# Row gathers moved from the routing to later blocks, and the gate product made for two expert blocks at a time, in a hybrid encoder layer

## The chip, the cores and the metric

The kernel runs on one core of a Trainium2 chip. The metric is the device time of one launch in microseconds; the kernel before takes 1673.27 us (median of three runs, 1672.91 to 1676.97). In the profile PE is TensorE (matrix products), DVE is VectorE, ACT is ScalarE, POOL is GpSimd and SP is the engine that issues most DMAs. PEld is PE's weight load.

## The reference, cut to what matters

One layer of an encoder on 512 tokens of width 1024. A mixing half (a long convolution and a gated recurrence) ends in a residual stream `h`. What this change touches is the second half, a retrieval over 16384 experts of one neuron each:

```python
def peer(x, wq, keys, u_tab, v_tab):
    q = (x @ wq).reshape(B, L, PEER_HEADS, 2, D_HALF)
    s = jnp.einsum('blhpd,hpkd->blhpk', q, keys)
    ts, ti = lax.top_k(s, K)
    ...
    experts = e1 * N_KEYS + e2
    g = jax.nn.softmax(cs, axis=-1)
    ...
        act = jax.nn.gelu(jnp.einsum('td,tkd->tk', xt, u_tab[et])) * gt
        return jnp.einsum('tk,tkd->td', act, v_tab[et])
```

Each token picks 8 x 16 experts; its output is the sum over them of gelu(x . u) times a gate g times v. The layer ends with a normalisation.

## The kernel before

**Two ways for the tokens.** For the first 384 tokens (`TD`) the kernel takes all 16384 experts, in 128 blocks of 128: a u block multiplies the block's u rows with the tokens (24 matmuls on PE into `ps_e`), ACT takes the gelu (L1019), a gate matrix that is zero for unchosen experts is multiplied in, and a v block adds the product times the block's v rows to the PSUM tiles `ob` (18 matmuls, L1045). For the other 128 tokens it fetches the 128 chosen u rows and later the 128 chosen v rows of each token from DRAM with indirect DMAs on POOL ("gathers", L1160, one row for each of 128 tokens, tile `rows`); DVE makes a dot product for each u gather (L1194, tile `junk`) and a multiply-add for each v gather (L1215, `acc2`, shown as `acc`). `GB` is 6, so five gathers are in flight ahead of the one in use.

**Weights.** Every matrix operand is fp16 in two parts. `w_load` fetches a block (tile `wf`, SP), `split` makes the high part on ACT (L119) and the rest on DVE (L120), tile `wh`, of which there are four; three `wf` buffers, six once the pool `gp` is open.

**Order of the work.** Every engine executes its instructions in the order in which the program wrote them. The loop over `self.seq` in `peer` writes u blocks 0 to 95 + LV, then a v block and a u block by turns, then v blocks alone. v blocks are taken in the order 96 to 127, then 0 to 95 (`vorder`). While the gates are still being worked out ("the routing": top-16 searches, one-hot matrices `oh` and `og` for eight tokens at a time, and matmuls `ps_gt` that turn them into the gate matrix, which ACT copies to `stg` and SP writes to DRAM, `gd`), each u block pulls a portion of the routing:

```python
                    self.pull(*self.PACE)
                    self.bud[0] -= 1.3 * gathers(self.GRATE[0])
```

`pull` writes routing instructions until 4.2 us of estimated DVE time (or of ACT time) are used up; each gather step is charged at 1.3 us. `gathers(rate)` adds the rate to a credit and writes one gather step for each whole unit; it starts once the row numbers `gidx` are there. When the routing is written out, the loop closes its pools, opens `vp` and the `ob` tiles, and asks for the first gate block (`gload`, four DMAs `gin<-gd`); from there the rate is `GRATE[1]` = 1.5 for each u and v block, and from the 33rd v block on it is (268 - steps done)/(E0 - 5), with E0 = 96.

**A v block's operand.** `pmul` multiplies the gelu (tile `sin`, reloaded from DRAM, or `hs`, still in SBUF) with the gates `gin` into `pf` (DVE, L1000); `phi` rounds it to fp16 on ACT (L1007, `pt`), `plo` makes the residue on DVE (L1011). At v block i the program writes `phi(i+2)`, `pmul(i+3)`, gathers, `plo(i+2)`. The last three v blocks' matmuls (`VT`) are written behind everything else, tile after tile of `ob`, each followed by `final`, the closing normalisation and the output's DMA.

Of the kernel before, what the change touches and what calls it, by code (L numbers as in the profile page):

```python
# [66 lines left out]
class Kernel:  # L67
# [276 lines left out]
    def front(self, xt, acc):  # L344
# [536 lines left out]
    def peer(self, acc):  # L881
        nc, tc, a = self.nc, self.tc, self.a
        E0, LV, VT = self.E0, self.LV, self.VT
        ctx = ExitStack()
# [87 lines left out]
        vp = None  # L972
        order = self.vorder
        gin, sin, pt, pf = {}, {}, {}, {}
        gs = {}

        def gload(k, q):
            if k < 128 // EB:
                b = order[EB * k] // EB
                if b not in gin:  # L980
                    gin[b] = vp.tile([128, NCH, EB, CH], F32, name="gin", bufs=2)
                cs = slice(q * NCH // 4, (q + 1) * NCH // 4)
                nc.sync.dma_start(gin[b][:, cs].rearrange("p c e t -> p c (e t)"),
                                  gd[cs, :, CH * EB * b:CH * EB * (b + 1)].rearrange("c p n -> p c n"))

        def sload(i):
            if i < 128 and order[i] < E0 and i % 2 == 0:
                b = order[i] // 2
                sin[b] = vp.tile([128, 2, TD], F32, name="sin", bufs=4)
                nc.sync.dma_start(sin[b], sd[b])  # L990

        def pmul(i):
            if i >= 128:
                return
            e = order[i]
            if i % EB in (3, 5, 7, 9):
                gload(i // EB + 1, (i % EB - 3) // 2)
            sload(i + 6)
            f = pf[i] = vp.tile([128, TD], F32, name="pf", bufs=2)
            nc.vector.tensor_tensor(f.rearrange("p (c t) -> p c t", c=NCH),  # L1000
                                    sin[e // 2][:, e % 2, :].rearrange("p (c t) -> p c t", c=NCH),
                                    gin[e // EB][:, :, e % EB, :], OP.mult)

        def phi(i):
            if i < 128:
                pt[i] = vp.tile([128, 2, TD], F16, name="pt", bufs=4)
                nc.scalar.activation(pt[i][:, 0, :], pf[i], AF.Copy)  # L1007

        def plo(i):
            if i < 128:  # L1010
                nc.vector.tensor_tensor(pt[i][:, 1, :], pf.pop(i), pt[i][:, 0, :], OP.subtract)  # L1011

        def gelu(e, ps):
            if e % 2 == 0:
# [39 lines left out]
        rate = None  # L1054
        for pos, (kind, e) in enumerate(seq):
            if kind == "u":
# [14 lines left out]
                if vp is None and (route not in self.bgq or e == E0 - 3):  # L1071
# [7 lines left out]
                    vp = ctx.enter_context(tc.tile_pool(name="vp", bufs=1, side="right"))  # L1079
# [9 lines left out]
                continue  # L1089
            i, vi = vi, vi + 1  # L1090
            if i == 0:
                for k in range(3):
                    pmul(k)
                    if k < 2:
                        phi(k)
                        plo(k)
            phi(i + 2)
            pmul(i + 3)
            if i >= 128 - E0:
                if rate is None:  # L1100
                    rate = (268 - self.gsteps) / (E0 - 5.0)
                gathers(rate)
            else:
                gathers(self.GRATE[1])
            plo(i + 2)
            w = self.w_get(u0 + pos)
            pp = pt.pop(i)
            if i >= 128 - VT:
# [7 lines left out]
            k = i - (128 - E0) - 20  # L1116
            if 0 <= k < 24:
                tt, c = divmod(k, 8)
# [24 lines left out]

    VT = 3
    E0 = 96
    LV = 5
    PACE = (4.2, 4.2)
    TB = 8
    GRATE = (0.8, 1.5)
    LAG = 2  # L1150
    GB = 6

# [388 lines left out]
```

## Time and profile before

| | before |
|---|---|
| runs | 1672.91, 1673.27, 1676.97 us |
| profiled execution | 1672.62 us, its span 1670.8 us |
| PE busy | 1610.5 us (96%) |
| DVE busy | 1407.0 us (84%) |
| ACT busy | 767.9 us (46%) |
| POOL busy | 379.6 us (23%) |
| moved by DMA | 435.06 MB, mean 260 GB/s |

The first u block begins at 578.5 us, the gathers at 674.6 us. In the order of PE's instructions the last `ps_gt` stands behind u block 89 and ends at 1004.5 us; the first v block begins at 1057.5 us, behind u block 101; from there to 1663.5 us v blocks follow. A share of busy time over the span says little here, since the stages differ; the rows below are taken stage by stage. In the rows of a stretch (a window), each engine has its busy time and its instructions, then PE's granted clock (1.00 is full), the mean busy share of the 16 DMA engines, and the GB/s they moved.

### The profile page before, as it was taken

The page shows a single profiled execution, that of the slowest core. Times are in us where ns is not written, and L with a number is a line of the kernel's source. Part 1 is how long each engine was busy: PE and PEld are TensorE (multiplying, and loading weights), DVE is VectorE, ACT ScalarE, POOL GpSimd, SP SyncE. Part 2 cuts the span into 40 slices and gives each one's busy share as a digit, 9 for nine tenths or more (in the row PEclk, how much of TensorE's full clock was granted, in tenths as well). Part 3 has the DMA queues.
Part 4 walks back from the last instruction along what each step waited for, and adds up shares of the span by engine and source line. Part 5 has one row for each costly group of instructions (what it writes and reads, how often), then busy time and mean ns, then how long its engine had stood idle before and what let it go on. Part 6 is the DMA issues. An engine that isn't in the chain of part 4 may idle for free. (4 is left out here: it accounts for less than half of the span.)

```text
span 1670.8 us, 25107 instructions
## 1 busy us (share of the span) xinstructions
PE 1610.5 (96%) x9451; PEld 901.7 (54%) x9451; DVE 1407.0 (84%) x2422; ACT 767.9 (46%) x1055; POOL 379.6 (23%) x357
## 2 busy tenths in 40 slices
PE   7999999899989988999998999999999999999998
PEld 5675666444435554666665665555554445544443
DVE  7736679987756799899999996998889998899975
ACT  5424278984431333444755763433333333333343
POOL 0000000002200000332222223555455333333400
PEclk9999999999999999999999999999999999999999
DMA  5342141229932246887888999999999999999951
GB/s 199 96 155 76 38 140 64 65 69 323 338 137 76 77 135 196 301 289 263 308 321 308 340 359 394 406 401 372 380 376 372 398 398 401 394 370 402 398 209 71
DMA packets 137738, 435.06 MB, mean 260 GB/s; under 512 B 13040, under 2 KB 37872, under 8 KB 134160
## 3 DMA queue, kind: packets, MB, share of 16 engines
q1 hardware_dynamic: 95360, 279.72, 46.4%
q0 software_dynamic: 42256, 153.73, 24.4%
q8 instruction: 74, 1.21, 0.3%
q14 instruction: 48, 0.39, 0.1%
HBM read 377.83 MB, written 55.57 MB: 259 GB/s over the span
## 5 line engine op out<-in xcount | busy, mean ns | idle before, releaser
L1045 PE MATMUL ob<-wh,pt 128*128 128x512 f16 x2304 | 505.9, 379 | 0.9 <-ACT pt L1007 0.9
L120 DVE SCALAR_TENSOR_TENSOR wh<-wf,wh 128x1024 f16<-128x1024 f32 (+1 forms) x324 | 389.8, 1207 | 96.8 <-ACT wh L119 96.5
L119 ACT ACTIVATE wh<-wf 128x1024 f16<-128x1024 f32 (+1 forms) x324 | 336.0, 1039 | 107.4 <-DMA wf<-in_peer_u 35.9
L1045 PEld LDWEIGHTS <-pt 128*128 128x128 f16 x2304 | 225.4, 98 | 264.3 <-ACT pt L1007 1.3
L126 PE MATMUL ps_e<-x,wh 128*128 128x384 f16 x1024 | 335.4, 328 | 16.3 <-DVE wh L120 16.3
L124 PE MATMUL ps_e<-x,wh 128*128 128x384 f16 x1024 | 335.1, 327 | 3.3 <-ACT gs L1019 2.3
L125 PE MATMUL ps_e<-x,wh 128*128 128x384 f16 x1024 | 335.4, 328 | 0.0
L1160 POOL DMA_INDIRECT rows<-in_peer_un,gidx x128 | 190.6, 1489 | 358.9 <-DVE junk L1194 314.8
L1160 POOL DMA_INDIRECT rows<-in_peer_v,gidx x128 | 163.2, 1275 | 235.3 <-DVE acc L1215 211.4
L126 PEld LDWEIGHTS <-wh 128*128 128x128 f16 x1376 | 135.1, 98 | 137.1 <-DVE wh L120 29.4
L125 PEld LDWEIGHTS <-wh 128*128 128x128 f16 x1376 | 135.1, 98 | 110.0 <-issue 6.3
L124 PEld LDWEIGHTS <-wh 128*128 128x128 f16 x1376 | 135.2, 98 | 104.0 <-issue 2.1
L1007 ACT ACTIVATE pt<-pf 128x384 f16<-128x384 f32 x128 | 66.8, 522 | 246.1 <-issue 217.7
L1215 DVE SCALAR_TENSOR_TENSOR acc<-rows,dots,acc 128x1024 f32<-128x1024 f32 x127 | 162.6, 1280 | 0.9
L1194 DVE SCALAR_TENSOR_TENSOR junk<-rows,xn 128x1024 f32<-128x1024 f32 x128 | 156.0, 1219 | 0.9
L331 PE MATMUL ps_p<-n,wh 128*128 128x264 f16 x960 | 112.5, 278 | 1.6 <-DVE wh L120 1.5
L1019 ACT ACTIVATE gs<-ps_e 128x384 f32<-128x384 f32 x96 | 47.0, 489 | 138.2 <-PE ps_e L126 126.1
L331 PEld LDWEIGHTS <-wh 128*128 128x128 f16 x960 | 94.4, 99 | 20.4 <-issue 3.5
L1369 ACT ACTIVATE stg<-ps_gt 128x512 f32<-128x512 f32 x96 | 93.0, 1079 | 19.8 <-PE ps_gt L1362 14.3
L1011 DVE TENSOR_TENSOR pt<-pf,pt 128x384 f16<-128x384 f32 x128 | 71.5, 559 | 12.8 <-ACT pt L1007 11.8
L124 PE MATMUL ps_p<-n,wh 128*128 128x512 f16 x192 | 73.6, 383 | 0.0
L125 PE MATMUL ps_p<-n,wh 128*128 128x512 f16 x192 | 73.4, 382 | 0.0
(288 smaller groups left out, 1922.7 us busy)
## 6 DMA issues: line engine op xcount, KB each, us to landing
wf<-in_peer_u SPq DMA_DIRECT2D x128, 512.0 KB, 5.9
wf<-in_peer_v SPq DMA_DIRECT2D x128, 512.0 KB, 10.6
gd<-stg SPq DMA_DIRECT2D x24, 1024.0 KB, 9.2
gin<-gd SPq DMA_DIRECT2D x32, 768.0 KB, 15.1
wf<-in_w_in SPq DMA_DIRECT2D x44, 512.0 KB, 3.6
sd<-gs SPq DMA_DIRECT2D x48, 384.0 KB, 7.1
sin<-sd SPq DMA_DIRECT2D x48, 384.0 KB, 12.6
pre<-ph POOLq DMA_DIRECT2D x18, 512.0 KB, 5.6
```

Of the source, the lines that this page charges most:

```text
L119: self.nc.scalar.activation(hi, src, AF.Copy, scale=s)
L120: self.nc.vector.scalar_tensor_tensor(lo, src, s, hi, op0=OP.mult, op1=OP.subtract)
L124: mm(ps, lh, rh, start=first, stop=False)
L125: mm(ps, lh, rl, start=False, stop=False)
L126: mm(ps, ll, rh, start=False, stop=last)
L331: nc.tensor.matmul(ps[:, h, :HL], x, n[:, y, c, h * HL:(h + 1) * HL], start=(c == 0 and x is lh and y == 0), stop=(c == 7 and x is ll))
L1011: nc.vector.tensor_tensor(pt[i][:, 1, :], pf.pop(i), pt[i][:, 0, :], OP.subtract)
L1045: mm(ob[tt][:, h, :], pp[:, x, sl], w[:, y, h * 512:(h + 1) * 512], start=first and k == 0, stop=last and k == 2)
L1160: self.nc.gpsimd.indirect_dma_start(out=r, out_offset=None, in_=table, in_offset=bass.IndirectOffsetOnAxis(ap=self.gidx[:, j:j + 1], axis=0))
L1194: nc.vector.scalar_tensor_tensor(junk, rows.pop(0), 1.0, self.xn, op0=OP.mult, op1=OP.mult, accum_out=self.dots[:, j:j + 1])
L1215: nc.vector.scalar_tensor_tensor(acc2, r, d, acc2, op0=OP.mult, op1=OP.add)
L1369: nc.scalar.activation(st[c][:, :, o:o + 4].rearrange("p e t -> p t e"), ps, AF.Copy, scale=S_P / S_G)
```

## The change

Four things are changed. (1) The gather rate during the routing, `GRATE[0]`, goes from 0.8 to 0.62 a u block. (2) The late rate becomes (263 - steps done)/(E0 - 4). (3) `pmul`, `phi` and `plo` work on two v blocks in one instruction of twice the width; at every second v block the program writes `phi(i+2)`, `pmul(i+4)`, gathers, `plo(i+2)`. `pf` stays at two buffers (now of two blocks each), `pt` goes from four of one block to three of two. The four `gload` calls of the next gate block come at blocks 2, 4, 6, 8 of 16 instead of 3, 5, 7, 9. (4) LV goes from 5 to 6, so one more u block stands ahead of the first v block.

```diff
-            if i % EB in (3, 5, 7, 9):
-                gload(i // EB + 1, (i % EB - 3) // 2)
+            if i % EB in (2, 4, 6, 8):
+                gload(i // EB + 1, i % EB // 2 - 1)
             sload(i + 6)
-            f = pf[i] = vp.tile([128, TD], F32, name="pf", bufs=2)
...
+            f = pf[i] = vp.tile([128, 2, TD], F32, name="pf", bufs=2)
+            nc.vector.tensor_tensor(f.rearrange("p e (c t) -> p e c t", c=NCH),
...
         def phi(i):
             if i < 128:
-                pt[i] = vp.tile([128, 2, TD], F16, name="pt", bufs=4)
-                nc.scalar.activation(pt[i][:, 0, :], pf[i], AF.Copy)
+                t = pt[i] = vp.tile([128, 2, 2, TD], F16, name="pt", bufs=3)
+                pt[i + 1] = t[:, :, 1, :]
+                nc.scalar.activation(t[:, 0], pf[i], AF.Copy)
...
-            phi(i + 2)
-            pmul(i + 3)
+            if i % 2 == 0:
+                phi(i + 2)
+                pmul(i + 4)
             if i >= 128 - E0:
                 if rate is None:
-                    rate = (268 - self.gsteps) / (E0 - 5.0)
+                    rate = (263 - self.gsteps) / (E0 - 4.0)
                 gathers(rate)
...
-    LV = 5
+    LV = 6
...
-    GRATE = (0.8, 1.5)
+    GRATE = (0.62, 1.5)
```

**DVE at the end of the routing.** L120 (`wh<-wf,wh`) is a weight block's split, `oh` and `og` (L1384 and L1388, L1389 and L1393 in the changed file) are routing, `junk` (L1194, now L1199) is a u gather's dot product; the last `og` is the end of the routing. Before:

```order
L1388 TENSOR_TENSOR og<-oh,gd_9113 128x2048
L1384 TENSOR_TENSOR oh<-iota,ed 128x2048
L1194 SCALAR_TENSOR_TENSOR junk,dots<-rows,xn 128x1024
L120 SCALAR_TENSOR_TENSOR wh<-wf,wh 128x1024
L1388 TENSOR_TENSOR og<-oh,gd_9113 128x2048
L1384 TENSOR_TENSOR oh<-iota,ed 128x2048
L1194 SCALAR_TENSOR_TENSOR junk,dots<-rows,xn 128x1024
L120 SCALAR_TENSOR_TENSOR wh<-wf,wh 128x1024
L1388 TENSOR_TENSOR og<-oh,gd_9113 128x2048
L1384 TENSOR_TENSOR oh<-iota,ed 128x2048
L120 SCALAR_TENSOR_TENSOR wh<-wf,wh 128x1024
L1388 TENSOR_TENSOR og<-oh,gd_9113 128x2048
```

The same place after the change:

```order
L1393 TENSOR_TENSOR og<-oh,gd_9016 128x2048
L1199 SCALAR_TENSOR_TENSOR junk,dots<-rows,xn 128x1024
L120 SCALAR_TENSOR_TENSOR wh<-wf,wh 128x1024
L1389 TENSOR_TENSOR oh<-iota,ed 128x2048
L1393 TENSOR_TENSOR og<-oh,gd_9016 128x2048
L120 SCALAR_TENSOR_TENSOR wh<-wf,wh 128x1024
L1389 TENSOR_TENSOR oh<-iota,ed 128x2048
L1393 TENSOR_TENSOR og<-oh,gd_9016 128x2048
L1389 TENSOR_TENSOR oh<-iota,ed 128x2048
L1393 TENSOR_TENSOR og<-oh,gd_9016 128x2048
L1199 SCALAR_TENSOR_TENSOR junk,dots<-rows,xn 128x1024
L120 SCALAR_TENSOR_TENSOR wh<-wf,wh 128x1024
```

Before, almost every split has a dot product ahead of it; now several splits have routing alone between them. Counted over the whole order, the last `og` stands behind 51 dot products before and behind 36 now, and five splits earlier. On PE the last `ps_gt` stands behind u block 85 instead of 89.

**ACT at the end of the routing.** `stg<-ps_gt` is the eviction of a gate matmul, `gs<-ps_e` the gelu of a u block, `wh<-wf` the high part of a weight block. Before:

```order
L1019 ACTIVATE gs<-ps_e 128x384
L1369 ACTIVATE stg<-ps_gt 128x4x128 x2
L119 ACTIVATE wh<-wf 128x1024
L1019 ACTIVATE gs<-ps_e 128x384
L1369 ACTIVATE stg<-ps_gt 128x4x128 x8
L1019 ACTIVATE gs<-ps_e 128x384
L119 ACTIVATE wh<-wf 128x1024 x2
```

After:

```order
L1023 ACTIVATE gs<-ps_e 128x384
L1374 ACTIVATE stg<-ps_gt 128x4x128 x4
L119 ACTIVATE wh<-wf 128x1024
L1023 ACTIVATE gs<-ps_e 128x384
L1374 ACTIVATE stg<-ps_gt 128x4x128 x6
L1023 ACTIVATE gs<-ps_e 128x384
L119 ACTIVATE wh<-wf 128x1024 x2
```

Ahead of the last u block's gelu in the old PSUM tiles there stood eight evictions, and now six.

**DVE at the first v blocks.** `pf<-hs,gin` is the product, `pt<-pf,pt` the residue. Before:

```order
L120 SCALAR_TENSOR_TENSOR wh<-wf,wh 128x1024
L1194 SCALAR_TENSOR_TENSOR junk,dots<-rows,xn 128x1024
L1000 TENSOR_TENSOR pf<-hs,gin 128x384
L1011 TENSOR_TENSOR pt<-pf,pt 128x384
L1000 TENSOR_TENSOR pf<-hs,gin 128x384
L1011 TENSOR_TENSOR pt<-pf,pt 128x384
L1000 TENSOR_TENSOR pf<-hs,gin 128x384 x2
L1194 SCALAR_TENSOR_TENSOR junk,dots<-rows,xn 128x1024 x2
L1011 TENSOR_TENSOR pt<-pf,pt 128x384
L120 SCALAR_TENSOR_TENSOR wh<-wf,wh 128x1024 x2
L1194 SCALAR_TENSOR_TENSOR junk,dots<-rows,xn 128x1024
```

After:

```order
L120 SCALAR_TENSOR_TENSOR wh<-wf,wh 128x1024
L1199 SCALAR_TENSOR_TENSOR junk,dots<-rows,xn 128x1024
L1001 TENSOR_TENSOR pf<-hs,gin 128x768 x2
L1014 TENSOR_TENSOR pt<-pf,pt 128x768
L1001 TENSOR_TENSOR pf<-hs,gin 128x768
L1199 SCALAR_TENSOR_TENSOR junk,dots<-rows,xn 128x1024 x2
L1014 TENSOR_TENSOR pt<-pf,pt 128x768
L120 SCALAR_TENSOR_TENSOR wh<-wf,wh 128x1024 x2
L1199 SCALAR_TENSOR_TENSOR junk,dots<-rows,xn 128x1024 x3
L120 SCALAR_TENSOR_TENSOR wh<-wf,wh 128x1024 x2
L1199 SCALAR_TENSOR_TENSOR junk,dots<-rows,xn 128x1024
```

Each product and residue now covers two v blocks (768 elements a partition instead of 384). Two wide products stand ahead of the first residue. Seventeen u blocks stand on PE between the last `ps_gt` and the first `ob` (u86 to u102), where twelve stood (u90 to u101). On DVE the last multiply-add of a v gather stands ahead of the product of v blocks 126 and 127 now; before it stood ahead of that of block 118, counted from 0.

## Rows read from the trace of the kernel before

**Rows 1.** Five stretches from the first u block to the end of the v blocks: from and to in us, length, then busy us (and instructions) of PE, PEld, DVE, ACT, POOL, then PE's clock, DMA share and GB/s.

```profile
578.50:674.00 95.50, 84.50 (x527) 48.90 (x525) 92.08 (x366) 35.69 (x50) 0.54 (x1) 1.00 0.53 173
674.00:1000.00 326.00, 316.73 (x2402) 204.60 (x2401) 318.95 (x544) 186.93 (x244) 93.95 (x57) 0.99 0.88 311
1000.00:1012.00 12.00, 8.43 (x71) 5.47 (x70) 6.37 (x10) 7.76 (x9) 2.58 (x2) 0.86 1.01 403
1012.00:1057.50 45.50, 43.60 (x268) 25.92 (x265) 31.93 (x45) 15.46 (x22) 20.81 (x17) 1.00 1.04 399
1057.50:1663.60 606.10, 605.93 (x2992) 295.59 (x2992) 535.12 (x672) 228.89 (x318) 236.49 (x181) 1.00 0.94 358
```

**Rows 2.** Who waited for whom from 674 to 1000 us: first all of PE's waits, then DVE's one; total us, times, longest.

```profile
PE ps_e L126 <- DVE wh L120: 5.3, 8, 1.0
PE ps_gt L1362 <- ACT stg L1369: 2.0, 6, 0.8
PE ps_gt L1362 <- DVE og L1388: 1.9, 2, 1.2
...
DVE wh L120 <- ACT wh L119: 3.2, 1, 3.2
```

**Rows 3.** Groups of DVE's instructions from 674 to 1004.6 us: the split of a weight block and the dot product of a u gather; busy us and mean ns of one behind the bar.

```profile
L120 DVE SCALAR_TENSOR_TENSOR wh<-wf,wh 128x1024 f16<-128x1024 f32 x69 | 84.0, 1220 | 3.3 <-ACT wh L119 3.2
L1194 DVE SCALAR_TENSOR_TENSOR junk<-rows,xn 128x1024 f32<-128x1024 f32 x52 | 63.3, 1216 | 0.0
```

**Rows 4.** DVE in order of time, behind the end of the routing: start, us, instruction, and in brackets the idle time before it. Two dot products in a row, then a split and what follows it.

```profile
1008.87 1.22 DVE L1194 SCALAR_TENSOR_TENSOR junk<-rows,xn 128x1024 f32<-128x1024 f32 x1
...
1010.13 1.23 DVE L1194 SCALAR_TENSOR_TENSOR junk<-rows,xn 128x1024 f32<-128x1024 f32 x1
...
1011.41 1.22 DVE L120 SCALAR_TENSOR_TENSOR wh<-wf,wh 128x1024 f16<-128x1024 f32 x1
1012.55 1.22 DVE L1194 SCALAR_TENSOR_TENSOR junk<-rows,xn 128x1024 f32<-128x1024 f32 x1
```

**Rows 5.** The end of the routing in order of time, first on PE, then on ACT.

```profile
1003.91 0.61 PE L1362 MATMUL ps_gt<-og,oh 128*128 128x128 f16 x8 [0.74 <-ACT stg L1369]
1006.80 0.32 PE L124 MATMUL ps_e<-x,wh 128*128 128x384 f16 x1 [2.28 <-ACT gs L1019]
...
1008.11 0.52 PE L124 MATMUL ps_e<-x,wh 128*128 128x384 f16 x1
...
1000.56 1.96 ACT L1369 ACTIVATE stg<-ps_gt 128x512 f32<-128x512 f32 x2 [2.85 <-PE ps_gt L1362]
1002.84 3.60 ACT L1369 ACTIVATE stg<-ps_gt 128x512 f32<-128x512 f32 x4 [0.32 <-DMA gd<-stg]
1006.24 0.52 ACT L1019 ACTIVATE gs<-ps_e 128x384 f32<-128x384 f32 x1
```

**Rows 6.** ACT in order of time: the gelu of two u blocks that follow each other where PE does not wait.

```profile
1020.38 0.49 ACT L1019 ACTIVATE gs<-ps_e 128x384 f32<-128x384 f32 x1 [2.47 <-PE ps_e L126]
...
1024.28 0.49 ACT L1019 ACTIVATE gs<-ps_e 128x384 f32<-128x384 f32 x1 [2.47 <-PE ps_e L126]
```

**Rows 7.** Pieces of the chain that ended last: start, us, what. A DMA of a weight block, the first product of the v blocks, two long pieces of v blocks, and the last instruction.

```profile
1018.33 17.08 DMA wf<-in_peer_u
...
1056.43 0.48 DVE pf L1000
...
1260.10 104.89 PE ob L1045 x486
...
1459.65 159.28 PE ob L1045 x738
...
1665.96 1.28 DVE rows L1141
```

**Rows 8.** PE's waits from 1012 to 1058 us.

```profile
PE ps_e L124 <- ACT hs L1019: 1.0, 1, 1.0
PE ob L1045 <- ACT pt L1007: 0.9, 1, 0.9
```

**Rows 9.** The instructions of the product, the rounding, the residue, and one DVE instruction of 1024 elements: duration ns min/median/max, first and last start, forms.

```profile
L1000 DVE TENSOR_TENSOR pf<-sin,gin x96: 548/552/555, 1268.6 to 1642.9; 128x384 f32<-128x384 f32 x96
...
L1007 ACT ACTIVATE pt<-pf x128: 507/524/527, 1056.9 to 1648.0; 128x384 f16<-128x384 f32 x128
...
L1011 DVE TENSOR_TENSOR pt<-pf,pt x128: 548/554/594, 1057.5 to 1648.5; 128x384 f16<-128x384 f32 x128
...
L1174 DVE TENSOR_TENSOR xg<-x x1: 1218/1218/1218, 674.4 to 674.4; 128x1024 f32<-128x1024 f16 x1
```

**Rows 10.** Two stretches of 20 us among the v blocks (columns as in rows 1), then the DMAs that load weight blocks, with KB each and median us from issue to landing: from 700 to 1000 us, and from 1260 to 1460 us.

```profile
1160.00:1180.00 20.00, 20.00 (x109) 10.49 (x108) 17.65 (x27) 7.64 (x11) 9.54 (x8) 1.00 0.93 331
...
1320.00:1340.00 20.00, 20.00 (x94) 9.05 (x93) 18.70 (x22) 7.36 (x10) 6.77 (x6) 1.00 1.03 406
...
wf<-in_peer_u SPq DMA_DIRECT2D x63, 512.0 KB, 6.1
...
wf<-in_peer_v SPq DMA_DIRECT2D x51, 512.0 KB, 12.9
```

**Rows 11.** DVE near the end, in order of time: the first addition behind the last v gather, and the last instruction of the gathered tokens' normalisation.

```profile
1619.86 0.69 DVE L1227 SCALAR_TENSOR_TENSOR acc<-ps_x,acc 128x512 f32<-128x512 f32 x1 [5.42 <-PE ps_x L1224]
...
1628.83 1.28 DVE L1141 SCALAR_TENSOR_TENSOR rows<-acc,fin,gfb 128x1024 f32<-128x1024 f32 x1
```

More of the change, by code (lines that the diff above doesn't have):

```diff
@@ L995, in pmul @@
             e = order[i]
-            if i % EB in (3, 5, 7, 9):
-                gload(i // EB + 1, (i % EB - 3) // 2)
+            if i % EB in (2, 4, 6, 8):
+                gload(i // EB + 1, i % EB // 2 - 1)
             sload(i + 6)
-            f = pf[i] = vp.tile([128, TD], F32, name="pf", bufs=2)
-            nc.vector.tensor_tensor(f.rearrange("p (c t) -> p c t", c=NCH),
-                                    sin[e // 2][:, e % 2, :].rearrange("p (c t) -> p c t", c=NCH),
-                                    gin[e // EB][:, :, e % EB, :], OP.mult)
+            f = pf[i] = vp.tile([128, 2, TD], F32, name="pf", bufs=2)
+            nc.vector.tensor_tensor(f.rearrange("p e (c t) -> p e c t", c=NCH),
+                                    sin[e // 2].rearrange("p e (c t) -> p e c t", c=NCH),
+                                    gin[e // EB][:, :, e % EB:e % EB + 2, :].rearrange("p c e t -> p e c t"), OP.mult)
         def phi(i):
             if i < 128:
-                pt[i] = vp.tile([128, 2, TD], F16, name="pt", bufs=4)
-                nc.scalar.activation(pt[i][:, 0, :], pf[i], AF.Copy)
+                t = pt[i] = vp.tile([128, 2, 2, TD], F16, name="pt", bufs=3)
+                pt[i + 1] = t[:, :, 1, :]
+                nc.scalar.activation(t[:, 0], pf[i], AF.Copy)
         def plo(i):
             if i < 128:
-                nc.vector.tensor_tensor(pt[i][:, 1, :], pf.pop(i), pt[i][:, 0, :], OP.subtract)
+                t = pt[i]
+                nc.vector.tensor_tensor(t[:, 1], pf.pop(i), t[:, 0], OP.subtract)
+                pt[i] = t[:, :, 0, :]
         def gelu(e, ps):
@@ L1091, in peer @@
             if i == 0:
[L1092 to L1096, printed above, removed]
-            phi(i + 2)
-            pmul(i + 3)
+                pmul(0)
+                pmul(2)
+                phi(0)
+                plo(0)
+            if i % 2 == 0:
+                phi(i + 2)
+                pmul(i + 4)
             if i >= 128 - E0:
                 if rate is None:
-                    rate = (268 - self.gsteps) / (E0 - 5.0)
+                    rate = (263 - self.gsteps) / (E0 - 4.0)
                 gathers(rate)
@@ L1104, in peer @@
                 gathers(self.GRATE[1])
-            plo(i + 2)
+            if i % 2 == 0:
+                plo(i + 2)
             w = self.w_get(u0 + pos)
```

## The prediction, made before the change was run

> **What bounds the kernel now.** I read the busy time of the engines by stretch first, since the kernel changes its limit from stage to stage. From 1057.5 us on, PE is busy 605.93 of 606.10 us [rows 1], and the chain that ended last runs there through v blocks in unbroken pieces of up to 159 us [rows 7]: that stage is PE at its full rate, and DVE has 71 us to spare in it. So a saving of DVE or ACT time there buys nothing; all that can be won lies ahead of 1057.5 us. Up to 674 us nothing changes, because no gather is written before the row numbers exist. What is left is three places.
>
> The routing, 674 to 1000 us: DVE is busy 318.95 of 326 us, PE 316.73 [rows 1]. The waits say which of them leads: most of PE's idle time is a wait for a weight split or an `og` from DVE, while DVE has one wait of 3.2 us [rows 2]. PE is idle 9.3 us there, and the clock of 0.99 takes between 0.5 and 1.5% of the 326 us for what it covers; I take the low end, 1.7 us. So DVE costs PE about 11 us in this stage.
>
> The end of the routing, 1000 to 1012 us: PE stops for 0.74 and 2.28 us behind ACT, which still evicts gate matmuls ahead of the gelu that frees the old PSUM tiles; behind the stop a matmul takes 0.52 us instead of 0.32 [rows 5]. Of the 12 us PE is idle 3.6 us, and the clock of 0.86 takes 1.7 more [rows 1].
>
> From 1012 to 1057.5 us: the DMA engines are at a share of 1.04 with 399 GB/s [rows 1], a weight block takes 17.08 us to land [rows 7], yet PE waits only 1.0 and 0.9 us [rows 8].
>
> **The change, part by part.**
> *The rate of 0.62.* On DVE 15 dot products leave the time ahead of the last `og` (51 against 36), and five splits with them, since the routing's budget refills what the gathers leave and ends four u blocks earlier. From start to start a dot product takes 1.26 us and a split 1.14 [rows 4] (their durations of 1216 and 1220 ns [rows 3] overlap a little with the next). That is 15 x 1.26 + 5 x 1.14 = 24.6 us less for DVE in this stage. PE loses four u blocks of 3.90 us each [rows 6], 15.6 us, which it does later instead, at the same price. Without any wait PE would need 326 - 11 - 15.6 = 299.4 us; DVE, if as full as now, 326 - 24.6 = 301.4. The two would be nearly level, and two engines that are level wait for each other a little in both directions, as the gate matmuls come in pairs in some u blocks and singly in others. I take 303.5 us, which leaves PE 4 us of its 11. The stage is then 22.5 us shorter and 15.6 us of it come back: gain 6.9 us. Bounds: 11 if no wait is left, 0.6 if each u block keeps its share of the wait (11 us over 69 splits [rows 3], four blocks gone).
>
> *The routing's end.* Six evictions instead of eight stand ahead of the last gelu; four take 3.60 us [rows 5], so two take 1.8, and PE's stop is 1.8 us shorter. Bounds: 5.3 us if stop and slow clock go altogether, 0 if what PE waits for is the write of `gd`, for which an eviction waited there too. I take 1.8.
>
> *Seventeen u blocks instead of twelve up to the first v block.* Of these, four are the ones moved and one is LV's, which only changes places with later work. DMA is the question here. With 1.5 gathers of 0.52 MB (128 x 1024 of 4 bytes), a weight block of 0.52 MB and, up to block 95, half of a 0.39 MB write of gelus (128 x 768 of 4 bytes), a block moves 1.5 MB, 3.8 us at 399 GB/s [rows 1] against PE's 3.90. The gate loads (four of 128 x 6 x 256 values, 0.79 MB) are the excess, 7.9 us, as before, and the weight buffers ahead hide it but for the 1.9 us of now [rows 8]. I leave these 1.9 us; bounds -1.9 (five blocks in which the loads catch up ahead of the first v block) and +4.
>
> *Two blocks per instruction.* 128x384 takes 552 ns for the product and 554 for the residue, 128x1024 takes 1218 [rows 9]; by the slope between, 768 elements take about 0.95 us. Per pair of v blocks DVE gets 2 x 0.95 in place of 4 x 0.55, 0.3 us less, 19 us over 64 pairs. It is worth nothing, since PE has no wait to lose in that stage. The cover that it would need if it were slower is DVE's 71 us [rows 1]. One place can feel it: two wide products stand ahead of the first residue, and the first v block starts when the first wide rounding (about 0.85 us, estimated as 524 ns [rows 9] and 384 elements more at the slope of DVE) follows the first wide product. Before, that was 0.55 + 0.52 us [rows 9]; now 1.8. If DVE is late there, as it was (the 0.9 us of [rows 8]), PE pays 0.7 us more; with five more blocks ahead of it I take 0.
>
> *The later rates and the tail.* Counted in the order, both files then have 1.2 multiply-adds per lone v block, so the demand for DMA per block is the same. The last one comes about 8 blocks later. Before, the first addition behind it began at 1619.86 us and the gathered tokens were finished at 1628.83 + 1.28 us [rows 11], far ahead of the end; now that chain of some 10 us ends beside the last three v blocks (3 x 3.9 us of matmuls). The last instruction at 1665.96 us belongs to `ob` [rows 7], and I leave its place. Cost 0, at most 3.
>
> The sum against the profiled execution: 1672.62 - 6.9 - 1.8 = 1663.9 us. The median of the runs lies 0.65 us above that execution, so 1664.6 us.
>
> *A rule that speaks against it.* Between 1320 and 1340 us the DMA engines stand at a share of 1.03 and move 406 GB/s [rows 10]; this is where the moved gathers' successors now land. The Trainium skill ("DMA: Bandwidth & Descriptors", section "Issuing engines are not separate DMA queues") says that transfers from different issuing engines run on the same 16 DMA engines and interleave, so POOL's gathers take their time from SP's weight loads. The trace agrees in so far as a weight block lands after 12.9 us there and after 6.1 us during the routing [rows 10]. Another section of that page ("Where 436 GB/s comes from") puts the limit for transfers from HBM at about 358 GB/s; the 399 and 406 GB/s of these rows are above it, so the measurement decides.
>
> **The rivals.**
> 1. *The wait stays per block.* `pull` gives each u block the same 4.2 us of estimated DVE time whether gathers or routing fill it. Then PE's wait per block stays, and only four blocks' share (0.6 us) and the 1.8 us go: 1671. For it: the budget is untouched. Against it: the order has 24.6 us of DVE work out of the stage for four blocks, 6.1 us a block, more than the 4.7 us that a block took on average (326 us over 69).
> 2. *DMA becomes the pace behind the routing (the other side).* The later stages get 15 gathers and four weight blocks, 10 MB, and two writes of gelus, 0.8 MB: 27 us at 399 GB/s [rows 1], while PE brings only 15.6 us of work along. If the transfers set the pace all the way, the sum is -22.5 - 1.8 + 27 = +2.7, 1676 us. It decides once a load lands later than six buffers can hide, about 6 x 3.9 = 23 us. For it: shares of 1.03. Against it: 12.9 us is half of that, PE waits nowhere, 331 GB/s are enough in some stretches [rows 10], and the last gathers have 8 more blocks to land in.
> 3. *Every stall goes:* 11 + 5.3 + 1.9 = 18 us, 1655. Against it: two level engines and pools that must still close.
>
> **How the numbers follow.** Forecast 0.70 (own range 1660 to 1668), rival 1 0.15, rival 2 0.06, rival 3 0.09. Within 0.3% (5 us, about what runs of this kernel can tell) means above 1668.3: rival 1 and a little of the forecast's edge. That gives faster 0.77, same 0.17, slower 0.06. The range goes to rival 1 above and halfway to rival 3 below: 1658 to 1671.5.
>
> **What would show it.** In the profile after: the last `ps_gt` near 980 us, the first `ob` near 1053 (8.7 us earlier, one u block later); PE's waits for DVE from 674 us to there at most 5 us, behind it below 2 us, and none among the v blocks; the wide product near 0.95 us; the end about 7.3 us behind the last matmul of `ob`. Wrong: PE waits for `wf` loads or for `rows` after 1060 us (rival 2), or 9 us of waits on DVE in the shorter routing (rival 1), or the closing of the pools as long as before.

## The result: slower by half a per cent, and the profile after

The changed kernel takes 1681.81 us (median of five runs, 1680.46 to 1686.59), the kernel before, beside it, 1673.03 (1672.70 to 1676.97). The ratio is 1.0055, its 95% interval 1.0042 to 1.0068. The forecast was 1664.6 us: the change went the other way. The profiled execution took 1680.49 us with a span of 1678.7; the forecast had 1663.9 us for it, so 16.6 us are to be found.

The stretches of the changed kernel, columns as in [rows 1]: the routing, its end, the u blocks up to the first v block, the v blocks, and 20 us out of the third.

```profile
674.00:977.00 303.00, 293.25 (x2241) 190.49 (x2240) 290.92 (x502) 177.47 (x232) 67.74 (x42) 0.99 0.83 291
977.00:990.00 13.00, 10.34 (x104) 7.49 (x103) 8.96 (x10) 8.98 (x12) 2.62 (x2) 1.00 0.85 295
990.00:1064.00 74.00, 63.54 (x376) 37.45 (x376) 48.43 (x66) 23.54 (x33) 32.07 (x23) 0.93 1.03 401
1064.00:1670.00 606.00, 606.00 (x2997) 296.03 (x2996) 529.68 (x561) 222.37 (x253) 267.32 (x189) 1.00 0.95 361
...
1020.00:1040.00 20.00, 9.73 (x46) 5.05 (x45) 9.68 (x14) 5.25 (x7) 6.87 (x6) 0.74 1.04 401
```

The v blocks are full to the last microsecond, as before. The third stretch is the one that changed its nature: PE is idle for 10.5 of 74 us, and from 1020 to 1040 us it is busy for less than half, at a clock of 0.74. PE's waits in the changed kernel, from 674 to 990 us (to be held against [rows 2]) and from 990 to 1070 us (against [rows 8]):

```profile
PE ps_e L126 <- DVE wh L120: 4.5, 6, 1.1
PE ps_gt L1367 <- ACT stg L1374: 4.3, 6, 2.9
PE ps_gt L1367 <- DVE og L1393: 1.3, 2, 1.0
...
PE ps_e L124 <- ACT gs L1023: 12.5, 2, 10.3
```

The waits on DVE, forecast to be at most 5 us, fell only from 5.3 + 1.9 us to 4.5 + 1.3. One stop of 10.3 us behind a gelu is new. (Of the 12.5 us, 2.28 are the stop at the routing's end, the same as in [rows 5].) ACT in order of time shows why the gelu came late: those of u87, u91 and u92, ahead of them an eviction of gate matmuls in the routing, and the high part (`wh`) that stands ahead of the last of these gelus:

```profile
923.99 1.95 ACT L1374 ACTIVATE stg<-ps_gt 128x512 f32<-128x512 f32 x2 [4.60 <-DMA gd<-stg]
...
998.20 0.49 ACT L1023 ACTIVATE gs<-ps_e 128x384 f32<-128x384 f32 x1 [2.42 <-PE ps_e L126]
...
1016.73 0.47 ACT L1023 ACTIVATE gs<-ps_e 128x384 f32<-128x384 f32 x1
1022.00 1.06 ACT L119 ACTIVATE wh<-wf 128x1024 f16<-128x1024 f32 x1 [4.80 <-DMA wf<-in_peer_u]
1031.28 0.49 ACT L1023 ACTIVATE gs<-ps_e 128x384 f32<-128x384 f32 x1 [8.22 <-DMA sd<-gs]
```

The gelu at 1031.28 waits for no matmul. It waits 8.22 us until the buffer it writes to has been saved to DRAM. That is not the whole stop of 10.3 us: ACT was ready for this gelu only at 1023.06 us, since the high part ahead of it had waited 4.80 us for its weight block. PE's last matmul before the stop ended at 1021.56 us, so by an estimate from these rows about 2 us of stop would have been left without the wait for the buffer, as much as the 1.0 + 0.9 of [rows 8]. Gelus of u blocks below 96 go by pairs into three `gs` buffers, each of which SP writes to `sd` before it can be used again; from block 96 on they go into four fresh `hs` buffers. The pair u86, u87 was complete at 998.20 + 0.49 us. When its write was issued, SP's queue tells (start, us of the issue itself, what):

```profile
990.27 0.66 SPq L1029 DMA_DIRECT2D sd<-gs  x1
1003.90 0.38 SPq L983 DMA_DIRECT2D gin<-gd  x1
...
1006.13 5.03 SPq L983 DMA_DIRECT2D gin<-gd  x1
1011.22 5.49 SPq L149 DMA_DIRECT2D wf<-in_peer_u  x1
...
1017.29 2.94 SPq L149 DMA_DIRECT2D wf<-in_peer_u  x1
1020.28 0.43 SPq L1029 DMA_DIRECT2D sd<-gs  x1
```

SP stood idle from 991 to 1004 us (the first gate load reads `gd` and waits 12.8 us for the last gate write to land), and behind it the gate loads and weight loads, which were written into the program first, took up to 5.5 us each to be issued, where an issue usually takes 0.3 to 0.5. So the write went out 21.6 us after the gelu was done. The chain that ended last shows the rest, and at its end the tail of the kernel:

```profile
1020.28 10.92 DMA sd<-gs
...
1031.28 0.50 ACT gs L1023
...
1031.82 0.48 PE ps_e L124
...
1673.87 1.28 DVE rows L1146
```

Before, the same queue was as late. SP of the kernel before, in order of time, and ACT's gelus of u91 (end of the first pair) and u95 there:

```profile
1022.82 7.21 SPq L983 DMA_DIRECT2D gin<-gd  x1
1030.12 4.35 SPq L149 DMA_DIRECT2D wf<-in_peer_u  x1
1034.51 0.44 SPq L1025 DMA_DIRECT2D sd<-gs  x1
```

```profile
1016.48 0.49 ACT L1019 ACTIVATE gs<-ps_e 128x384 f32<-128x384 f32 x1 [2.41 <-PE ps_e L126]
...
1032.08 0.49 ACT L1019 ACTIVATE gs<-ps_e 128x384 f32<-128x384 f32 x1 [2.47 <-PE ps_e L126]
```

There the write went out 17.5 us after its gelu (1034.51 against 1016.48 + 0.49), and nobody waited for it: the routing ended with u89, three pairs (90 to 95) were left below 96, and there are three buffers. With the rate of 0.62 the routing ends with u85, five pairs are left, and the fourth and fifth need a buffer back. A second stop, in the routing, has grown: an eviction waits 4.60 us for a gate write (`gd`), and PE 2.90 behind it, where PE's longest wait for an eviction was 0.8 us [rows 2] (PE in order of time, with the stop at the routing's end):

```profile
925.08 1.01 PE L1367 MATMUL ps_gt<-og,oh 128*128 128x128 f16 x8 [2.90 <-ACT stg L1374]
...
990.20 0.32 PE L124 MATMUL ps_e<-x,wh 128*128 128x384 f16 x1 [2.28 <-ACT gs L1023]
```

Where the 16.6 us lie: the first u block behind the routing starts at 990.20 us, 16.6 earlier than at 1006.80 [rows 5], where 22.5 + 1.8 = 24.3 were forecast: 7.7 us missing. From there to the first `ob` before it was 1057.5 - 1006.8 = 50.7 us for 12 blocks, 3.9 more than 12 x 3.90; now it is 1069.3 - 990.2 = 79.1 us for 17, 12.8 more than 17 x 3.90: 8.9 us missing. 7.7 + 8.9 = 16.6, and behind the first `ob` nothing is lost.

### The profile page after: what moved, and what is told of

It is laid out like the page before. It is cut to its first block, busy times and chain, and to the rows that moved or that the text cites. A ratio compares the mean times of both kernels' runs of the same rounds, so it can differ in the third digit from the quotient of the medians.

```text
span 1678.7 us, 24893 instructions
## 1 busy us (share of the span) xinstructions
PE 1610.4 (96%) x9451; PEld 901.9 (54%) x9451; DVE 1395.2 (83%) x2294; ACT 761.2 (45%) x991; POOL 396.3 (24%) x357
## 3 DMA queue, kind: packets, MB, share of 16 engines
q0 software_dynamic: 42256, 153.73, 24.3%
## 5 line engine op out<-in xcount | busy, mean ns | idle before, releaser
L120 DVE SCALAR_TENSOR_TENSOR wh<-wf,wh 128x1024 f16<-128x1024 f32 (+1 forms) x324 | 389.9, 1207 | 131.0 <-ACT wh L119 122.6
L126 PE MATMUL ps_e<-x,wh 128*128 128x384 f16 x1024 | 336.0, 328 | 15.6 <-DVE wh L120 15.4
L124 PE MATMUL ps_e<-x,wh 128*128 128x384 f16 x1024 | 336.0, 328 | 12.5 <-ACT gs L1023 12.5
L1165 POOL DMA_INDIRECT rows<-in_peer_v,gidx x128 | 180.1, 1407 | 225.7 <-DVE acc L1220 201.9
L1199 DVE SCALAR_TENSOR_TENSOR junk<-rows,xn 128x1024 f32<-128x1024 f32 x128 | 156.1, 1220 | 1.4
L124 PE MATMUL ps_p<-n,wh 128*128 128x512 f16 x192 | 73.4, 382 | 0.0
L126 PE MATMUL ps_p<-n,wh 128*128 128x512 f16 x192 | 73.3, 382 | 0.0
L125 PE MATMUL ps_p<-n,wh 128*128 128x512 f16 x192 | 73.3, 382 | 0.0
L1389 DVE TENSOR_TENSOR oh<-iota,ed 128x2048 f16<-128x2048 f16 x48 | 58.5, 1218 | 3.4 <-PE ps_gt L1367 3.4
```

The source lines that it names most:

```text
L120: self.nc.vector.scalar_tensor_tensor(lo, src, s, hi, op0=OP.mult, op1=OP.subtract)
L124: mm(ps, lh, rh, start=first, stop=False)
L125: mm(ps, lh, rl, start=False, stop=False)
L126: mm(ps, ll, rh, start=False, stop=last)
L1165: self.nc.gpsimd.indirect_dma_start(out=r, out_offset=None, in_=table, in_offset=bass.IndirectOffsetOnAxis(ap=self.gidx[:, j:j + 1], axis=0))
L1199: nc.vector.scalar_tensor_tensor(junk, rows.pop(0), 1.0, self.xn, op0=OP.mult, op1=OP.mult, accum_out=self.dots[:, j:j + 1])
```

## The experiments

The theory after the result (the *buffers theory*): the loss is the stop on a `gs` buffer, which is caused by SP's order and by too few buffers. Rivals: too little bandwidth of the DMA engines, and the two-block instructions. Twelve kernels, all computing the whole output; the medians and ratios below are against runs of the kernel before on the same chip. The last three columns are PE's waits in us from 674 to 1070 us, in total: for a gelu into `gs`, for an eviction (`stg`), for a split (`wh`).

| kernel | median us | ratio (95% interval) | gs | stg | wh |
|---|---|---|---|---|---|
| changed kernel | 1681.81 | 1.0055 (1.0042 to 1.0068) | 12.5 | 4.3 | 4.5 |
| a1_rate_only | 1682.39 | 1.0060 (1.0044 to 1.0077) | 13.0 | 6.3 | 4.4 |
| a2_old_rate | 1673.37 | 1.0007 (0.9997 to 1.0016) | 2.3 | 3.7 | 5.3 |
| a3_hs_from_92 | 1672.98 | 0.9998 (0.9988 to 1.0007) | 2.3 | 6.5 | 4.5 |
| a4_half_gathers_in_between | 1677.74 | 1.0034 (1.0020 to 1.0049) | 7.5 | 3.8 | 4.5 |
| b1_both_on_act | 1671.96 | 0.9992 (0.9982 to 1.0001) | 7.5 | 1.3 | 4.5 |
| b2_gd_on_act | 1666.91 | 0.9961 (0.9948 to 0.9974) | 2.9 | 1.3 | 4.5 |
| b3_sd_on_act | 1673.05 | 1.0000 (0.9990 to 1.0009) | 5.4 | 3.6 | 4.5 |
| b4_before_both_on_act | 1672.92 | 0.9994 (0.9984 to 1.0004) | 2.9 | 4.5 | 5.5 |
| b5_only_gd_on_act | 1677.43 | 1.0033 (1.0020 to 1.0045) | 12.2 | 1.3 | 4.5 |
| c1_gate_loads_apart | 1677.08 | 1.0022 (1.0012 to 1.0031) | 6.2 | 6.9 | 4.4 |
| c3_fast_gate_loads_apart | 1669.70 | 0.9980 (0.9970 to 0.9989) | 2.9 | 1.3 | 4.5 |
| c2_pace_4_0 | 1661.85 | 0.9933 (0.9917 to 0.9950) | 2.9 | 4.0 | none |

### Which part of the change costs the time

**a1_rate_only**: the kernel before with the new rate alone.

```diff
-    GRATE = (0.8, 1.5)
+    GRATE = (0.62, 1.5)
```

> The kernel before with one number changed: the gather rate during the routing is 0.62 instead of 0.8; single-width products, LV 5 and the old late rate stay. Theory 'buffers' (the routing ends four u blocks earlier, so that ten gelu blocks instead of six must go through the three write-back buffers gs while SP is held up by the gate loads): the stop of some 10 us in which ACT waits for the write of sd is there, and with one u block less ahead of the first v block the time is 1679 to 1684 us. Rival 'width' (the two-block instructions, LV 6 or the later gate loads cost the time): no such stop, 1665 to 1673 us.

**a2_old_rate**: the changed kernel with the old rate; the two-block instructions stay.

```diff
-    GRATE = (0.62, 1.5)
+    GRATE = (0.8, 1.5)
```

> The changed kernel with the gather rate during the routing back at 0.8; two-block products, LV 6 and the new late rate stay. Theory 'buffers': no stop on the write of sd, 1670 to 1675 us, the same as the kernel before within 0.2%. Rival 'width': as slow as the changed kernel, 1679 to 1683 us.

Measured: 1682.39 and 1673.37 us. The rate alone is the whole loss; the two-block instructions, LV and the late rate together change nothing that the intervals show. The stop is there without them; PE's wait in a1_rate_only:

```profile
PE ps_e L124 <- ACT gs L1019: 13.0, 2, 10.7
```

### Buffers, bandwidth, or the queue

**a3_hs_from_92**: behind the routing the fresh `hs` buffers are used from block 92 on instead of 96. No DMA is added or taken away, the order stays; only the buffer that a gelu needs is another.

```diff
-                gs[0] = xp.tile([128, 2, TD], F32, name="gs", bufs=3) if e < E0 else \
+                gs[0] = xp.tile([128, 2, TD], F32, name="gs", bufs=3) if e < (E0 if vp is None else 92) else \
```

> The changed kernel, but the gelus of u blocks 92 to 95 go to the four buffers of the later pool (the ones that blocks 96 and up use), so that the three gs buffers serve only u blocks up to 91. Theory 'buffers': ACT's wait for the write of sd and PE's stop of 10.3 us go, with the slow clock behind it 12 us in all: 1668 to 1672 us. Rival 'bandwidth' (the DMA engines are full from the end of the routing on, and the stop is only where that shows): PE waits for weight blocks instead, and no more than 4 us are won: 1677 to 1682 us.

**a4_half_gathers_in_between**: half as many gathers in the u blocks behind the routing.

```diff
-                    gathers(self.GRATE[1])
+                    gathers(self.GRATE[1] if vi else 0.75)
```

> The changed kernel with 0.75 instead of 1.5 gathers for each u block between the routing's end and the first v block; what is left is spread over the lone v blocks by the late rate. It takes 13 gathers, 6.8 MB or 17 us of DMA at 400 GB/s, out of the stage with the stop. Rival 'bandwidth': the stop goes, 1668 to 1672 us. Theory 'buffers': the write of sd still stands in SP's queue behind the four gate loads, but these are issued sooner with less traffic, so the stop is shortened to between 2 and 7 us, 1672 to 1678 us.

**b3_sd_on_act**: the write of a `gs` buffer is issued from ACT's queue, right behind the gelu that fills it, in place of SP's.

```diff
-                self.dq.append((sd[e // 2], gs[0]))
+                nc.scalar.dma_start(sd[e // 2], gs[0])
```

> The changed kernel, with the writes of the gelus (sd) issued from ACT's queue right behind the second gelu of a pair, no longer from SP behind its weight and gate loads; three gs buffers as before. If the write comes late because it stands in SP's queue behind loads that wait ('queue'), the stop of 10.3 us goes without another buffer: 1669 to 1674 us. If it comes late because the DMA engines are full ('bandwidth': it took 10.9 us from issue to landing), most of the stop stays: 1677 to 1682 us.

Measured: a3 1672.98, b3 1673.05: each gives the 8.8 us back to within 0.1. In a3 the bytes and their order are those of the changed kernel, so the loss isn't bandwidth as such: it hangs on the missing buffer. The stretch in which PE was busy for 9.73 of 20 us, in a3:

```profile
1020.00:1040.00 20.00, 19.42 (x119) 11.53 (x118) 10.06 (x14) 5.94 (x9) 6.67 (x6) 1.00 1.04 397
```

The DMA engines are as full as before (share 1.04, 397 GB/s), and PE works through. a3 missed the range expected of it, 1668 to 1672, by a microsecond: the stop on the gate writes stayed, at 4.7 us in its profiled execution. How long that stop is differs by execution and not by edit: the changed kernel, a3, a4 and c1 are the same program up to the routing's end, and PE's longest wait for an eviction was 2.9, 4.7, 2.4 and 5.4 us in their profiles. b3 says that the order of the queue is the other condition: the same write, to the same DMA engines, issued on time, and the longest stop is 2.7 us. Either repair removes the loss, so it takes both, the late write and the missing buffer. The Trainium skill ("DMA: Bandwidth & Descriptors", section "Issuing engines are not separate DMA queues") says that starting DMAs from several engines saves only the time of starting them, usually small beside the transfer. The write's own issue was indeed short here, 0.43 us against 10.92 to land; what another engine's queue saved is the 21.6 us for which it stood behind other issues on SP.

a4 halves the stop without removing it (1677.74 us). What it did can be read on SP: the third gate load and the two weight loads that follow it took 0.45, 3.06 and 2.59 us to issue, where they took 5.03, 5.49 and 2.94, and the write went out at 1013.66 us in place of 1020.28. It then took longer to land: the gelu that needs its buffer begins at 1028.42 us, 14.8 us after the issue, where the changed kernel's begins 11.0 us after it, so of the 6.6 us gained at the issue the buffer was back only 2.9 us sooner; the rest of the shorter stop is that PE came to it 2.2 us later in this execution (1023.76 us against 1021.56).

```profile
1006.78 0.45 SPq L983 DMA_DIRECT2D gin<-gd  x1
1007.28 3.06 SPq L149 DMA_DIRECT2D wf<-in_peer_u  x1
...
1011.03 2.59 SPq L149 DMA_DIRECT2D wf<-in_peer_u  x1
1013.66 0.97 SPq L1029 DMA_DIRECT2D sd<-gs  x1
```

So how full the DMA engines are goes with the length of an issue on SP: the share from 1003 to 1021 us was 0.98 with 346 GB/s in a4, and 1.04 with 392 in the changed kernel. The Trainium skill ("Perfetto Trace Analysis", section "DMA Instruction — HWDGE (DVE, Sync)") fits this: the time shown for an issue runs until the sequencer is free again, and the engines may begin before all descriptors are made if these don't fit in the buffer. No run here isolates that buffer.

**c1_gate_loads_apart**: the other cause of the late write, the place of the gate loads in the program. The four are spread over ten blocks.

```diff
-                elif vp is not None and e in (e0 + 1, e0 + 2, e0 + 3):
-                    gload(0, e - e0)
+                elif vp is not None and e in (e0 + 1, e0 + 4, e0 + 7, e0 + 10):
+                    if e > e0 + 1:
+                        gload(0, (e - e0 - 1) // 3)
```

> The changed kernel with the four gate loads behind the routing asked for three u blocks apart (at the routing's end and 4, 7 and 10 blocks later) instead of one block apart; the first v block needs them 17 blocks later. If it is the gate loads in a row that hold SP's queue and with it the write of the gelus, the stop of 10.3 us shrinks to under 3 us: 1670 to 1674 us. If the weight loads and gathers alone fill the DMA engines so far that the write is late anyway: 1678 to 1682 us.

Measured: 1677.08 us, between the two expectations. The longest stop falls from 10.3 to 3.6 us, yet ACT still waits 14.9 us in all for writes of `gs`, because weight loads now hold the queue as long: two of them for 9.60 us, with what lies between them, and a single issue for 8.03:

```profile
1009.12 9.60 SPq L149 DMA_DIRECT2D wf<-in_peer_u  x2
1018.78 2.29 SPq L1029 DMA_DIRECT2D sd<-gs  x1
...
1023.27 8.03 SPq L149 DMA_DIRECT2D wf<-in_peer_u  x1
```

So the gate loads' place is about half of the loss (4.7 of 8.8 us by the medians), and moving them doesn't free the queue.

### The second stop, and what is left without stops

**b2_gd_on_act**: a3, and the gate write issued from ACT's queue behind the eviction.

```diff
-                gs[0] = xp.tile([128, 2, TD], F32, name="gs", bufs=3) if e < E0 else \
+                gs[0] = xp.tile([128, 2, TD], F32, name="gs", bufs=3) if e < (E0 if vp is None else 92) else \
...
-                        self.dq.append((gd[c, :, :128 * CH], st.pop(c).rearrange("p e t -> p (e t)")))
+                        nc.scalar.dma_start(gd[c, :, :128 * CH], st.pop(c).rearrange("p e t -> p (e t)"))
```

> The kernel with the gelus of blocks 92 to 95 in other buffers (1672.98 us), and with the write-backs of the gates (gd) issued from ACT's queue right behind their last eviction. Theory 'write-back of the gates': the stop near 920 to 940 us (PE 4.7 us behind ACT, ACT 6.6 us behind the write of gd, and the clock at 0.83 for 20 us behind it) comes from writes that stand in SP's queue; it goes, and with it 5 to 8 us: 1665 to 1668 us. Rival 'DVE': the routing is as long as DVE makes it, the stop only moves, and no more than 2 us are won: 1671 to 1673 us.

**b5_only_gd_on_act**: the second of the two edits alone, on the changed kernel.

```diff
-                        self.dq.append((gd[c, :, :128 * CH], st.pop(c).rearrange("p e t -> p (e t)")))
+                        nc.scalar.dma_start(gd[c, :, :128 * CH], st.pop(c).rearrange("p e t -> p (e t)"))
```

> The changed kernel with only the write-backs of the gates (gd) issued from ACT's queue; the gelus' writes stay on SP and the three gs buffers stay. If the two stops are independent and add up, the stop of 920 to 940 us goes and the one of 10.3 us stays: 1674 to 1677 us (1681.8 less the 6 us that the same step gave where the other stop was gone). If they share one cause, so that freeing SP's queue from the gates also lets the gelus' writes through: 1666 to 1671 us.

Measured: 1666.91 us, in the range expected, and 1677.43, half a microsecond above that of two independent stops. With both stops gone the changed kernel is 6 us faster than the kernel before. PE's waits in b2, and its stretch from 920 to 940 us (16.54 us busy at a clock of 0.83 in the changed kernel):

```profile
PE ps_e L126 <- DVE wh L120: 4.5, 6, 1.1
PE ps_e L124 <- ACT gs L1023: 2.9, 1, 2.9
PE ps_e L124 <- ACT hs L1023: 1.9, 1, 1.9
...
PE ps_gt L1367 <- ACT stg L1374: 1.3, 5, 0.3
```

```profile
920.00:940.00 20.00, 19.45 (x181) 13.60 (x180) 19.83 (x19) 14.12 (x18) 3.35 (x2) 1.00 0.96 356
```

The two repairs are worth 8.8 us (a3) and 4.4 us (b5) alone, and 14.9 together. That is 1.7 more than their sum, within what the intervals leave open (about 2 us on each), so the two stops add up as far as these runs can tell.

**b1_both_on_act**: both writes on ACT's queue, on the changed kernel, with its three `gs` buffers. **b4_before_both_on_act**: the same two edits on the kernel before.

```diff
-                self.dq.append((sd[e // 2], gs[0]))
+                nc.scalar.dma_start(sd[e // 2], gs[0])
...
-                        self.dq.append((gd[c, :, :128 * CH], st.pop(c).rearrange("p e t -> p (e t)")))
+                        nc.scalar.dma_start(gd[c, :, :128 * CH], st.pop(c).rearrange("p e t -> p (e t)"))
```

> The changed kernel with both kinds of write-back (sd and gd) issued from ACT's queue, buffers unchanged. If both stops come from the order in SP's queue: 1664 to 1669 us, what the prediction had forecast for the change. If an issue on ACT itself waits for room in the DMA rings, ACT's waits move there and PE still stops behind ACT: 1672 to 1680 us.

> The kernel before (rate 0.8, single products, LV 5) with both kinds of write-back issued from ACT's queue. It has six gelu blocks, not ten, between the routing's end and the fresh buffers and no stop on sd; its waits on gd are 5.5 us on ACT in all and cost PE 3.3 us at most. If the gain of the write-backs on ACT's queue belongs to the changed kernel's stops: 1670 to 1674 us here. If it helps the kernel whatever its order: 1664 to 1668 us.

Measured: 1671.96 and 1672.92 us. b4 gains nothing: what waits on these writes the kernel before has cost no time that the medians show. b1 lies between the two expectations, 5 us behind b2. ACT works in order, too: its issue of a `gs` write came at 1014.34 us, 10 us after the gelu that fills it (1003.84 + 0.49), and the weight's high part behind it 10.39 us late:

```profile
1014.34 0.33 ACTq L1025 DMA_DIRECT2D sd<-gs  x1
1014.72 1.06 ACT L119 ACTIVATE wh<-wf 128x1024 f16<-128x1024 f32 x1 [10.39 <-DMA gin<-gd]
```

The issue itself took 0.33 us. The profile ends the wait at the landing of a gate load; why a write issued from ACT waits for that load, no run here shows.

**c3_fast_gate_loads_apart**: b2 with the gate loads spread as in c1 (both diffs stand above).

> The fastest version so far (1666.9 us) with the gate loads three u blocks apart as well. It still loses 1.9 us at 1029 us and has ACT waiting up to 5.7 us for a weight block behind the gate loads. If the gate loads in a row cause that: 1664 to 1666 us; if not: 1666 to 1668 us.

Measured: 1669.70 us, a miss for both: 2.8 us slower than b2. The wait on `hs` is gone, but PE now waits at the first v block, since on DVE the first product stands behind a split, and ACT waited 4.12 us for that split's weight block (PE there):

```profile
1056.23 2.03 PE L1049 MATMUL ob<-wh,pt 128*128 128x512 f16 x8 [2.10 <-ACT pt L1009]
```

That trade explains a result level with b2, not one behind it. The profiled execution of c3 took 1667.51 us, less than b2's 1668.0, so the profile doesn't show where its median loses the 2.8 us; this stays open. All that follows is that moving the gate loads gains nothing once the buffers are there.

### Does the wait on DVE come from the budget per block?

**c2_pace_4_0**: b2 with 4.0 us of estimated DVE time per u block in place of 4.2.

```diff
-    PACE = (4.2, 4.2)
+    PACE = (4.0, 4.2)
```

> The fastest version so far (gelus of 92 to 95 in other buffers, gd on ACT's queue, 1666.9 us) with a budget of 4.0 instead of 4.2 us of DVE time for each u block's portion of the routing, so that the routing ends behind u block 90 instead of 85. It still has 4.5 us of PE waiting for splits on DVE. If that wait is set per block by the budget (rival 1 of the prediction), it falls below 1.5 us: 1663 to 1665 us. If DVE's work is uneven inside the routing and each burst costs PE whatever the mean: the wait stays above 3 us, 1666 to 1668 us.

Measured: 1661.85 us, 0.9933 (0.9917 to 0.9950) of the kernel before and better than the 1663 to 1665 expected; it beats both kernels. The routing now ends behind u90, one block later than in the kernel before, and PE's wait on `wh`, 4.4 to 5.5 us in every other kernel, isn't in the list of 674 to 1070 us:

```profile
PE ps_gt L1367 <- ACT stg L1374: 4.0, 6, 2.2
PE ps_e L124 <- ACT gs L1023: 2.9, 1, 2.9
```

That wait isn't the whole gain of 5.1 us over b2, and part of it moved: the wait for evictions rose from 1.3 to 4.0 us. The budget also holds before the gathers begin, in u blocks that the table doesn't cover: from 570 to 674 us PE's wait for splits is 11.0 us in the kernels before and after and in b2, and 8.3 in c2. From 570 us to the end of the routing, PE's waits come to 20.9 us in b2 and 16.0 in c2, and that difference, 4.9 us, is about the gain.

## Why the prediction was wrong, step by step

**The step that failed** is the sum's term for the seventeen u blocks: "I leave these 1.9 us; bounds -1.9 ... and +4". The stage lost 12.8 us where the forecast had left it the 3.9 of the kernel before: 8.9 us more. Bytes were set against bandwidth and weight buffers, and by that reckoning the term was right: the DMA engines moved 401 GB/s, and in a3 and b2, with the same demand, nothing like the stop appears. What the step left out is a buffer that has to be written out before its next use, by a queue that works in order: ACT waited 8.22 us for it, and a3, which only gives it another buffer, gets 8.8 us back. The four moved blocks were counted as PE's work (15.6 us, done "at the same price"); nobody counted that they carry two more pairs of gelus into the place where SP is blocked, three buffers for five pairs. Both numbers stood in the code, `bufs=3` and `E0`. The 12.8 us of that stage are 10.3 us of stop, some 2 of them a late weight block and not the buffer, and 2.5 us of slow clock after it: from 1031.8 to 1036.8 us the granted clock was 0.50 (1.2 GHz), and matmuls took 0.32 us start to start in place of 0.16. In b2 the same stage takes 1056.86 - 986.78 = 70.1 us; the forecast's was 17 x 3.90 + 3.9 = 70.2.

**The rate of 0.62 and the routing's end**, 6.9 + 1.8 us forecast. The changed kernel gained 16.6 - 15.6 = 1.0 us there. In b2, without the stop on the gate write, the gain is 20.0 - 15.6 = 4.4 us. So of the 7.7 us missing here, 3.4 are that stop, of which the prediction has nothing, and 4.3 are terms mis-sized by half. (b1, b5 and c3, also without that stop, start the first u block 0.4 to 1.4 us sooner than b2, so the half is rough.) DVE did lose the work: from 674 to 989 us it has 38 dot products, where there were 52 [rows 3], and four splits fewer. Part of the work saved became idle time of DVE, 8.6 us in two groups of waits, where it had been 3.2 [rows 2]; the second group is the stop on the gate write as DVE sees it, and is gone in b2:

```profile
DVE wh L120 <- ACT wh L119: 5.2, 2, 3.2
DVE oh L1389 <- PE ps_gt L1367: 3.4, 5, 2.3
```

PE's wait for splits stayed at 4.5 us, and c2 shows what sets it: it goes with 0.2 us less budget per block. That is rival 1, the wait that stays per block: its 0.6 + 1.8 = 2.4 us are nearer to the 4.4 than the forecast's 8.7. The argument held against it, 6.1 us of DVE work gone per block, was about the average over blocks, and the budget fills each block to the same mark whatever the average. At the routing's end six evictions did go ahead of the last gelu in place of eight, and PE's stop was 2.28 us as before, so the term of 1.8 us failed. ACT shows why:

```profile
986.22 3.61 ACT L1374 ACTIVATE stg<-ps_gt 128x512 f32<-128x512 f32 x4 [1.12 <-PE ps_gt L1367]
```

The last four evictions, 3.6 us in a row, stand directly ahead of the gelu in both kernels [rows 5]. In the changed one ACT comes to them early and waits 1.12 us for PE's own gate matmuls; the two evictions saved lay ahead of that wait. It isn't the gate writes that set it: in b2, which issues them from ACT, the stop is still 2.9 us. The slow clock of [rows 5] did not follow the stop in this execution (1.00 from 990 to 995 us), but that isn't a gain of the change: a4 is the same program up to there, has the same stop of 2.28 us, and its clock was 0.66 from 990 to 995; in a3 it was 0.66 from 994 to 999.

**Two blocks per instruction**: right. The tiles `pf` and `pt` of the changed kernel (ns min/median/max, first and last start), and the matmuls that use them:

```profile
L1009 ACT ACTIVATE pt<-pf x64: 826/827/843, 1066.5 to 1647.3; 128x768 f16<-128x768 f32 x64
L1014 DVE TENSOR_TENSOR pt<-pf,pt x64: 945/951/958, 1067.4 to 1655.6; 128x768 f16<-128x768 f32 x64
L1001 DVE TENSOR_TENSOR pf<-sin,gin x48: 949/951/1002, 1272.4 to 1640.8; 128x768 f32<-128x768 f32 x48
...
L1049 PE MATMUL ob<-wh,pt x2304: 379/379/379, 1069.3 to 1671.0; 128*128 128x512 f16 x192
```

0.95 and 0.85 us were forecast. (By the prediction's own working, 524 ns and 384 elements more at DVE's slope of 1.04 ns, the rounding comes to 0.92; that its 0.85 lies nearer to the 0.83 measured is luck.) PE has no wait from the first `ob` on, and a2 against before is 1.0007 with 1 inside its interval.

**The later rates and the tail**: right. From the first to the last `ob` matmul nothing is lost, and the last instruction ends 7.3 us behind the products, in the chain of `ob` as before; the gathered tokens are finished at 1663.94 + 1.29 us, ahead of it.

**Rival 2**, the one on the slower side, had the right sign, and a time of 1676, by a mechanism that didn't occur: transfers that set the pace among the v blocks. There the share is 0.95 and PE is never idle. **Rival 3** fell with its condition.

**The signs that were to show it**: the last `ps_gt` near 980 us came at 987.9, the first `ob` near 1053 at 1069.3, and the waits on DVE, "at most 5 us", were 5.8. One of the signs of being wrong did show, the stop at the closing of the pools, as long as before (2.28 us), but it is not where the loss lies. The text's main sign for a wrong forecast, loads of `wf` or `rows` after 1060 us, would have missed the cause: it sat before 1060, in a write.

## What to carry to other kernels

When work is moved across a point where a queue is blocked (here SP, waiting for the last gate write and then for slow issues), count the buffers that this queue must empty, and how many uses of them now fall behind the point: three buffers for three pairs cost nothing, three for five cost about 9 us. Read the issue time of each DMA on the in-order queue, not only bytes and landing times, and ask which write stands behind the loads. And where a budget per block sets the mix of two engines' work, taking work out elsewhere doesn't shorten a wait that the budget makes; change the budget.

## What the runs showed of the hardware beyond that

A single issue on SP's queue took 0.33 to 0.5 us in most places and up to 8.03 us (c1) while the DMA engines stood at a share of 1.03 to 1.04; with half the gathers (a4) the three that had taken 5.03, 5.49 and 2.94 us took 0.45, 3.06 and 2.59. An issue on ACT's queue can hold up ACT's work: in b1 it came 10 us after the gelu, and ACT's next work 10.39 us late. A stop of 10.3 us was followed by 5 us of matmuls at half rate, with a granted clock of 0.50 (1.2 GHz). A stop of 2.28 us at the routing's end was followed by the slow clock in the profiles of the kernel before (0.53 from 1008 to 1011 us), of a3 and of a4, but not in that of the changed kernel (1.00 from 990 to 995 us), which is the same program up to there as a3 and a4.
